# One engine instead of two empties PSUM, and the second pair of score tiles leaves in one store

## The chip, the core and the metric

The kernel runs on one NeuronCore of a Trainium2 chip; the other cores are idle. The metric is device microseconds (us) for one execution, as a median over several runs. The engines named below are PE (TensorE, matmuls), DVE (VectorE), ACT (ScalarE), POOL (GpSimd) and SP (SyncE, which here only issues DMAs). "SPq" and "ACTq" are the instruction queues of SP and ACT where they issue DMAs.

## The reference

```
q, k: (8, 8, 512, 64) float32          # batch, heads, seq, dim
out = einsum('bhqd,bhkd->bhqk', q, k) * (1 / sqrt(64))
out: (8, 8, 512, 512) float32
```

Each of the 64 batch-and-head pairs gives a 512 x 512 matrix of scaled dot products. There is no softmax. 16.78 MB are read and 67.11 MB are written, so the output is four times the input.

## The kernel before

**Tiles.** The work is cut into `ALL` = 16 tiles, numbered `g`. A tile is 4 MB of output: 16 matmuls of 128 x 512 results, in two rounds `x` of eight PSUM banks `i`. PSUM (`ps`) has eight banks of 128 x 512 float32, so one round fills all of PSUM. An evacuation takes four banks at once (`W` = 4, a 128 x 2048 block), multiplies by the scale and writes to SBUF. A tile has four evacuations, `n` = 0 to 3; `n` = 0 and 2 are the low four banks of the two rounds, `n` = 1 and 3 the high four.

**Buffers.** `big` in SBUF has `UNITS` = 4 slots of one tile each. Tile `g` goes to slot `g % 4`. The same four slots take the inputs first: all loads are issued at the start, one after another, to these slots (line 83, and two half loads at line 72). POOL casts them to bf16 in `xb` (line 126), DVE transposes them into `kT` (keys, line 191) and `qz` (queries, line 196) in eight sets `b` of two tiles each.

**Order on each engine.** Nothing is scheduled automatically; each engine has its own program, and semaphores tie them together.

- SP issues the loads and then the stores (lines 85 to 101). Tiles 0 to 3 are stored one by one (line 95): an even tile when PE has done the matmuls that imply its evacuation (`pe`), an odd tile when its last evacuation has counted `out` up. From tile 4 on two tiles leave in one store of 8 MB (line 98), issued when the odd one is done.
- PE runs a loop of four passes over four tiles each (lines 135 to 158). Before the first matmul of an even tile it waits for `free0` or `free1`, which counts that the store that used these two slots has landed, that the preceding pair has been evacuated, and that DVE has turned the operands. Within a tile, each four banks wait for their evacuation (`low0`, `low1`, `high0`, `high1`).
- ACT does all evacuations of tiles 0 to 3 and, from tile 4 on, those with `n` = 0, 2 and 3 (line 170).
- DVE does the evacuation `n` = 1 of tiles 4 to 15 (line 168), placed between its transposes: that of the even tile after the keys of a set, that of the odd tile between the second and third transpose of the queries, the last two at the end. The choice stands in `evacuate`:

```python
by_vector = g >= UNITS and n == 1
```

So two slots of `big` (a pair of tiles) are filled while the two other slots drain to memory.

Of the kernel before, what the change touches and what calls it, by code (L numbers as in the profile page):

```python
# [5 lines left out]
def kernel(  # L6
# [5 lines left out]
    nc = tc.nc  # L12
    B, H, S, D = q.shape
    scale = 1.0 / (D ** 0.5)
    P = 128
    Q = 32
    UNITS = B // 2
# [6 lines left out]
    W = 4  # L24
    ALL = 2 * B
# [11 lines left out]
    sem = {name: nc.alloc_semaphore(name) for name in names}  # L37
# [14 lines left out]
    bigs = [big[:, n] for n in range(UNITS)]  # L52
# [3 lines left out]
    ps = nc.alloc_psum_tensor("ps", [P, RO, S], f32)[:]  # L56
# [6 lines left out]
    def xf(v):  # L63
        return bigs[v].rearrange("p x i k -> p (x i k)").rearrange("p (x s c) -> p x s c", x=2, s=2)
# [6 lines left out]
    for s, queue in enumerate((nc.sync, nc.scalar)):  # L71
        first_load = queue.dma_start(
            out=xf(0)[:, 0, s].rearrange("p (x c) -> p x c", x=2), in_=k_0[s]
# [7 lines left out]
    for n in range(1, 2 * UNITS):  # L81
        v, x = divmod(n, 2)
        nc.sync.dma_start(out=xf(v)[:, x].rearrange("p s c -> p (s c)"), in_=(k_r, q_r)[x][v]
                          ).then_inc(load_sems[n], 16)
    for g in range(ALL):
        if g % 2:
            nc.sync.wait_ge(sem["out"], g // 2 + 1)
        elif g < UNITS:
            nc.sync.wait_ge(sem["pe"], 4 * g + 6)
        else:  # L90
            continue
        dst = out_r[g // 4, g // 2 % 2]
        free = sem[f"free{g // 2 % 2}"]
        if g < UNITS:
            nc.sync.dma_start(out=dst[:, g % 2 * 2:g % 2 * 2 + 2],  # L95
                              in_=bigs[g].rearrange("p x i k -> p x (i k)")).then_inc(free, 16)
        else:
            nc.sync.dma_start(out=dst, in_=big[:, g % UNITS - 1:g % UNITS + 1].rearrange(
                "p n x i k -> p (n x) (i k)")).then_inc(free, 32)
        if g % 2 and g < ALL - 1:  # L100
            nc.sync.sem_inc(sem[f"free{1 - g // 2 % 2}"], 1)  # L101
# [5 lines left out]
    for v in range(UNITS):  # L107
# [3 lines left out]
        for x in range(2):  # L111
            if v or x:
                nc.gpsimd.wait_ge(load_sems[2 * v + x], 16)
            for s in range(2):
                if v == x == 0:
                    nc.gpsimd.wait_ge(halves[s], 16)
                src = xf(v)[:, x, s]
                dst = xb[:, slot(v, x)]
                if x == 0:
                    src = src.rearrange("p (w e d) -> p w e d", e=2, d=D)  # L120
                    dst = dst[:, s * J // 2:(s + 1) * J // 2].rearrange("p w d e -> p w e d")
                else:
                    src = src.rearrange("p (jj e i d) -> p jj e i d", e=2, i=RO, d=D)
# [10 lines left out]
    pe = nc.tensor  # L134
    with pe.Fori(0, ALL // 4):
        for t in range(4):
# [10 lines left out]
            for x in range(2):  # L147
                for i in range(RO):
                    if (x, i) in waits:
                        name, count = waits[x, i]  # L150
# [5 lines left out]
                    elif (x, i) in takes:  # L156
                        name, count = takes[x, i]
                        ins.then_inc(sem[name], -count)


    def evacuate(g, n):
        x, i = n // 2, n % 2 * W
        by_vector = g >= UNITS and n == 1
        engine = nc.vector if by_vector else nc.scalar
        engine.wait_ge(sem["pe"], 4 * g + n + 1)
        to, src = bigs[g % UNITS][:, x, i:i + W], ps[:, i:i + W]
        if by_vector:
            freed = nc.vector.tensor_scalar_mul(out=to, in0=src, scalar1=scale)  # L168
        else:
            freed = nc.scalar.mul(out=to, in_=src, mul=scale)  # L170
        name = "out" if g % 2 and n == 3 else f"{('low', 'high')[n % 2]}{g // 2 % 2}"
        freed.then_inc(sem[name], 1)

    for g in range(ALL):
        for n in range(4):
            if g < UNITS or n != 1:
                evacuate(g, n)

# [1 line left out]
    def turn_keys(b, y, heads=slice(0, G)):  # L182
        s = b % 2 * 2 * Q
        out = kw[2 * y * Q:2 * (y + 1) * Q, b % 2 * G:(b % 2 + 1) * G]
        src = xw[s:s + 2 * Q, slot(b // 2, 0), :, y * Q:(y + 1) * Q]
        if b < 2:
            out = out[:, heads].rearrange("d g (m w) -> d g w m", m=Q)
            src = src.rearrange("p (g w) d -> p g w d", g=G)[:, heads]
        else:
            out = out.rearrange("d g (m w) -> d w m g", w=J)  # L190
        return nc.vector.transpose(out=out, in_=src)  # L191

    def turn_queries(b, y, h, rows=slice(0, RO)):
        s = (b % 2 * 2 + h) * Q
        d = (2 * y + h) * Q
        return nc.vector.transpose(  # L196
            out=qw[d:d + Q, b % 2 * G:(b % 2 + 1) * G, rows, h * Q:(h + 1) * Q].rearrange(
                "d g i (m jj) -> d i jj m g", jj=JJ),
            in_=xw[s:s + Q, slot(b // 2, 1), :, y * Q:(y + 1) * Q].rearrange(
                "p (i jj) d -> p i jj d", i=RO)[:, rows])  # L200

    sides = [(y, h) for y in range(2) for h in range(2)]
# [12 lines left out]
    for b in range(1, SETS):  # L215
        if b >= 2:
            nc.vector.wait_ge(sem["pe"], 8 * (b - 1))
        if b % 2 == 0:
            nc.vector.wait_ge(sem["ready"], b + 1)
        for y in range(2):  # L220
            turn_keys(b, y)
        if b > 2:
            evacuate(2 * b - 2, 1)
        if b % 2 == 0:
            nc.vector.wait_ge(sem["ready"], b + 2)
        for n, (y, h) in enumerate(sides):
            if b > 2 and n == 2:
                evacuate(2 * b - 1, 1)
            last = turn_queries(b, y, h)
        last.then_inc(sem["turned" if b == 1 else f"free{b % 2}"], 1)  # L230
    for g in (ALL - 2, ALL - 1):
        evacuate(g, 1)


# [28 lines left out]
```

## Time and profile before

| | us |
|---|---|
| median of 4 runs | 200.69 (200.49 to 200.76) |
| profiled execution, its own time | 200.51 |
| profiled execution, span from first to last instruction | 199.1 |

| engine | busy us | share of the span | what it does |
|---|---|---|---|
| DVE | 127.2 | 64% | 54 transposes, 12 evacuations, one memset |
| ACT | 95.9 | 48% | 52 evacuations |
| PE | 80.2 | 40% | matmuls |
| POOL | 38.9 | 20% | casts, all in the first quarter |
| DMA | | 99% of 16 engines (97.7% + 1.3%) | loads and stores, 421 GB/s over the span |

| group | mean ns of one | count |
|---|---|---|
| ACT evacuation, 128x2048 float32, line 170 | 1883 | 52 |
| DVE evacuation, 128x2048 float32, line 168 | 2292 | 12 |
| DVE transpose of queries, 32x1024, line 196 | 2014 | 28 |
| DVE transpose of keys, 64x1024, line 191 | 1932 | 14 |

The profile is of one execution. Busy time is summed over the span, and says nothing by itself of what holds up the end; the chain that ended last and the waits do. All DMA rows carry a share of the core's 16 DMA engines: near 1.00 means that all of them were moving data. The share can come out a little over 1 in a short stretch, because a packet is counted where it begins.

### The profile page before, as it was taken

Reading aid. Unit: us, or ns where it says so; the run is one execution under the profiler, and the core shown is the slowest. Engines: PE = TensorE matmul, PEld = TensorE weight load, DVE = VectorE, ACT = ScalarE, POOL = GpSimd, SP = SyncE. Lnnn points to the kernel's source line nnn. Section 1 sums busy time; section 2 is a strip of 40 time slices with the busy share of each in tenths; the row PEclk is TensorE's granted clock in tenths of the full one; section 3 lists DMA queues with packets and bytes.
Section 4 is the critical chain, followed back from the end, with each engine's and each line's share of the span. In section 5 each row is a group of like instructions: output and inputs, shape, how many; then the busy total and the mean of one; then the engine's idle time right before and its main releaser. Section 6 shows DMA issues by size and latency. Waiting matters only on the chain.

```text
span 199.1 us, 726 instructions
## 1 busy us (share of the span) xinstructions
PE 80.2 (40%) x252; PEld 23.6 (12%) x256; DVE 127.2 (64%) x67; ACT 95.9 (48%) x53; POOL 38.9 (20%) x20
## 2 busy tenths in 40 slices
PE   0000357556514752575167516660756076600000
PEld 0000021121101110221022102110211021100000
DVE  4248999999370799589959895999399513400000
ACT  2000049959960776177526752773377337720000
POOL 0399999698000000000000000000000000000000
PEclk9999999979995899589957975998599859955555
DMA  6999999999999999999999999999999999999997
GB/s 201 431 438 441 435 425 421 421 412 425 438 444 425 428 425 438 444 421 428 425 438 441 428 426 425 435 438 431 428 428 431 431 441 425 425 425 431 425 431 309
DMA packets 5809, 83.90 MB, mean 421 GB/s; under 512 B 304, under 2 KB 304, under 8 KB 816
## 3 DMA queue, kind: packets, MB, share of 16 engines
q1 hardware_dynamic: 5536, 82.84, 97.7%
q10 hardware_dynamic: 272, 1.05, 1.3%
q14 instruction: 1, 0.01, 0.0%
HBM read 16.78 MB, written 67.11 MB: 421 GB/s over the span
## 4 chain that ended last, share of the span: by engine, by line
DMA 41%; ACT 30%; PE 8%; DVE 4%; POOL 2%; issue 1%; SPq 0%
DMA out_dram<-big 36%; ACT big L170 30%; PE ps L152 8%; DMA big<-in_q_dram 6%; DVE qz L196 4%; POOL xb L126 2%; SPq L95 0%; SPq L101 0%
## 5 line engine op out<-in xcount | busy, mean ns | idle before, releaser
L170 ACT ACTIVATE big<-ps 128x2048 f32<-128x2048 f32 x52 | 94.6, 1883 | 77.8 <-PE ps L152 77.8
L152 PE MATMUL ps<-kT,qz 128*128 128x512 bf16 x252 | 80.2, 455 | 93.4 <-DMA out_dram<-big 37.1
L196 DVE STREAM_TRANSPOSE qz<-xb 32x1024 f32<-32x1024 f32 (+1 forms) x36 | 65.2, 1811 | 1.2 <-POOL xb L126 0.7
L168 DVE TENSOR_SCALAR big<-ps 128x2048 f32<-128x2048 f32 x12 | 27.5, 2292 | 30.2 <-PE ps L152 30.2
L152 PEld LDWEIGHTS ps<-kT,qz 128*128 128x128 bf16 x256 | 23.6, 110 | 149.5 <-DMA out_dram<-big 40.1
L126 POOL CAST xb<-big 128x2048 bf16<-128x2048 f32 x16 | 38.7, 2472 | 10.1 <-DMA big<-in_k_dram 7.5
L191 DVE STREAM_TRANSPOSE kT<-xb 64x1024 f32<-64x1024 f32 (+1 forms) x18 | 31.5, 1747 | 11.0 <-POOL xb L126 6.5
L203 DVE MEMSET qz<- 128x4096 uint32 x1 | 3.5, 3472 | 2.9 <-PEq L77 2.9
L170 ACT ACT_TABLE_LOAD x1 | 1.3, 1283 | 2.0 <-PEq L77 2.0
L247 POOL MEMSET const-float32-0.0<- 128x1 f32 x1 | 0.1, 99 | 0.2 <-issue 0.2
L247 POOL MEMSET const-bfloat16-1.0<- 128x1 bf16 x1 | 0.1, 102 | 0.0
L247 POOL MEMSET const-uint8-127<- 128x1 uint8 x1 | 0.1, 102 | 0.0
L247 POOL MEMSET const-float32-1.0<- 128x1 f32 x1 | 0.1, 99 | 0.0
## 6 DMA issues: line engine op xcount, KB each, us to landing
out_dram<-big SPq DMA_DIRECT2D x6, 8192.0 KB
out_dram<-big SPq DMA_DIRECT2D x4, 4096.0 KB
big<-in_q_dram SPq DMA_DIRECT2D x4, 2048.0 KB, 23.9
big<-in_k_dram SPq DMA_DIRECT2D x3, 2048.0 KB, 23.9
big<-in_k_dram SPq DMA_DIRECT2D x1, 1024.0 KB, 7.2
big<-in_k_dram ACTq DMA_DIRECT2D x1, 1024.0 KB, 8.7
```

The costliest lines, as they stand in the source:

```text
L126: cast = nc.gpsimd.tensor_copy(out=dst, in_=src)
L152: ins = pe.matmul(out=ps[:, i], lhsT=qz[:, 2 * t + x, i], rhs=kT[:, 2 * t + x], start=True, stop=True)
L168: freed = nc.vector.tensor_scalar_mul(out=to, in0=src, scalar1=scale)
L170: freed = nc.scalar.mul(out=to, in_=src, mul=scale)
L191: return nc.vector.transpose(out=out, in_=src)
L196: return nc.vector.transpose(out=qw[d:d + Q, b % 2 * G:(b % 2 + 1) * G, rows, h * Q:(h + 1) * Q].rearrange("d g i (m jj) -> d i jj m g", j ...
L203: nc.vector.memset(qz, 0.0).then_inc(sem["zeroed"], 1)
L247: nc = _bacc.Bacc("TRN2", target_bir_lowering=False, num_devices=1)
```

## The change

Tiles 2 and 3 leave in one store, as the later pairs do, so SP issues two single stores and seven pairs instead of four and six. All evacuations are done by ACT, in the order of tiles; those with `n` = 1 of tiles 4 to 15 move from DVE to ACT. DVE keeps the memset and the transposes, in the same order. The waits of the moved evacuations (on `pe`) and what they count up (`high0`, `high1` for the next wait of PE) are the same as before. Only the index of the first pair and the even tile's wait differ in SP's program: the wait for `pe` at tile 2 is gone.

```diff
     for g in range(ALL):
         if g % 2:
             nc.sync.wait_ge(sem["out"], g // 2 + 1)
-        elif g < UNITS:
+        elif g == 0:
             nc.sync.wait_ge(sem["pe"], 4 * g + 6)
         else:
             continue
         dst = out_r[g // 4, g // 2 % 2]
         free = sem[f"free{g // 2 % 2}"]
-        if g < UNITS:
+        if g < 2:
             nc.sync.dma_start(out=dst[:, g % 2 * 2:g % 2 * 2 + 2],
...
-    def evacuate(g, n):
-        x, i = n // 2, n % 2 * W
-        by_vector = g >= UNITS and n == 1
-        engine = nc.vector if by_vector else nc.scalar
-        engine.wait_ge(sem["pe"], 4 * g + n + 1)
-        to, src = bigs[g % UNITS][:, x, i:i + W], ps[:, i:i + W]
-        if by_vector:
-            freed = nc.vector.tensor_scalar_mul(out=to, in0=src, scalar1=scale)
-        else:
-            freed = nc.scalar.mul(out=to, in_=src, mul=scale)
-        name = "out" if g % 2 and n == 3 else f"{('low', 'high')[n % 2]}{g // 2 % 2}"
-        freed.then_inc(sem[name], 1)
-
     for g in range(ALL):
         for n in range(4):
-            if g < UNITS or n != 1:
-                evacuate(g, n)
+            x, i = n // 2, n % 2 * W
+            nc.scalar.wait_ge(sem["pe"], 4 * g + n + 1)
+            freed = nc.scalar.mul(out=bigs[g % UNITS][:, x, i:i + W], in_=ps[:, i:i + W], mul=scale)
+            name = "out" if g % 2 and n == 3 else f"{('low', 'high')[n % 2]}{g // 2 % 2}"
+            freed.then_inc(sem[name], 1)
...
         for y in range(2):
             turn_keys(b, y)
-        if b > 2:
-            evacuate(2 * b - 2, 1)
         if b % 2 == 0:
             nc.vector.wait_ge(sem["ready"], b + 2)
-        for n, (y, h) in enumerate(sides):
-            if b > 2 and n == 2:
-                evacuate(2 * b - 1, 1)
+        for y, h in sides:
             last = turn_queries(b, y, h)
         last.then_inc(sem["turned" if b == 1 else f"free{b % 2}"], 1)
-    for g in (ALL - 2, ALL - 1):
-        evacuate(g, 1)
```

## The prediction

> **What bounds the kernel now.** I read the page's slices first. All 16 DMA engines are busy from the second slice to the last but one, at 412 to 444 GB/s, while every compute engine has gaps.
>
> ```profile
> DMA  6999999999999999999999999999999999999997
> GB/s 201 431 438 441 435 425 421 421 412 425 438 444 425 428 425 438 444 421 428 425 438 441 428 426 425 435 438 431 428 428 431 431 441 425 425 425 431 425 431 309
> HBM read 16.78 MB, written 67.11 MB: 421 GB/s over the span
> ```
>
> The reader should see that no slice in the middle has a hole. 83.9 MB at the 432 GB/s of the middle are 194.2 us of a span of 199.1 us. So an engine's time counts only if it leaves the DMA engines without work. Whether it comes near to that is read from the chain that ended last.
>
> ```profile
> 81.84 1.90 PE ps L152 x4
> ...
> 93.67 3.65 ACT big L170 x2
> 97.32 0.02 issue
> 97.34 23.62 DMA out_dram<-big
> 120.96 0.05 issue
> 121.00 1.90 PE ps L152 x4
> ```
>
> A pair's round has three steps. PE starts when the store that used these two slots has landed (81.84). PSUM is filled and emptied eight times. Then SP issues the pair's store (97.34), which lands 23.62 us later. But 8.39 MB need only 19.4 us at 432 GB/s: the new store first queues behind the other pair's. That queueing is the reserve. To see how large it is I took the PE starts and the store issues from the timeline and asked for the stretch between them:
>
> ```profile
> 41.97:58.18 16.21, 9.69 (x31) 2.88 (x32) 12.02 (x7) 14.27 (x8) 7.28 (x4) 0.90 1.00 430
> 62.39:77.85 15.46, 9.66 (x32) 2.89 (x32) 11.60 (x6) 11.04 (x6) 0.00 (x0) 0.89 1.01 432
> 81.84:97.34 15.50, 10.02 (x31) 2.94 (x32) 12.35 (x7) 11.04 (x6) 0.00 (x0) 0.86 1.01 434
> 101.34:117.22 15.88, 10.55 (x32) 3.01 (x32) 12.34 (x7) 10.94 (x6) 0.00 (x0) 0.82 1.01 432
> 121.00:136.17 15.17, 9.43 (x31) 2.89 (x32) 12.57 (x7) 10.96 (x6) 0.00 (x0) 0.91 1.00 431
> 140.50:155.97 15.47, 9.66 (x32) 2.87 (x32) 11.97 (x7) 11.04 (x6) 0.00 (x0) 0.88 1.00 429
> 160.09:175.62 15.53, 10.15 (x31) 2.97 (x32) 4.58 (x2) 10.94 (x6) 0.00 (x0) 0.83 1.00 427
> ```
>
> Each row is a pair from its first matmul to its store's issue: start and end, length, busy time of PE, PEld, DVE, ACT and POOL, granted clock, DMA share, GB/s. The first row is tiles 2 and 3, which ACT already empties alone (x8); in the others ACT does six and DVE two. So the trace of before contains the changed stage. The starts are 19.45, 19.50, 19.66, 19.50 and 19.59 us apart (62.39, 81.84, 101.34, 121.00, 140.50, 160.09): the time that a pair takes to drain. The reserve, from an issue to the next start, is 3.99, 4.00, 3.78, 4.33 and 4.12 us.
>
> **The change, part by part.** *Twelve evacuations leave DVE.* 12 x 2.292 = 27.5 us go, and DVE's transposes of a set end earlier. They were in time already: the queries of the next pair end at 78.75 (74.73 + 4.02), PE starts at 81.84. Worth nothing; the 8.5 us that PE waits for DVE's evacuations turn into waits for ACT.
>
> *Twelve evacuations go to ACT.* 12 x 1.883 = 22.6 us are added in ACT's queue, two per pair, with the third and fourth evacuation of each tile behind them, and behind those PE's refill of the banks and the pair's store. ACT takes eight in a row in 14.27 us, one every 1.77 us, since one begins before the former has quite ended:
>
> ```profile
> 43.89 14.27 ACT L170 ACTIVATE big<-ps 128x2048 f32<-128x2048 f32 x8 [2.43 <-PE ps L152]
> ```
>
> With 1.92 us for the first four matmuls that makes the 16.21 us of the first row. That stage ran beside DVE transposes and POOL casts, at half clock in its first microseconds like the later ones, so I take it as it is. The difference to the other rows is 0.75, 0.71, 0.33, 1.04, 0.74 and 0.68 us, mean 0.71: the two engines overlap little, because PE can refill only four banks at a time. At worst, with no overlap of two ACT instructions, the stage is 1.92 + 8 x 1.883 = 16.98 us. At best it is as long as now.
>
> The Trainium skill speaks against the change here: "PSUM — Partial Sum Buffer", section "Specifications (TRN2)", says that ScalarE and VectorE can read PSUM in parallel at full bandwidth when they use different banks. By that rule alone a pair's 8 x 1.883 us could be halved by two engines, so that one alone would take 7.5 us longer per pair; this overruns the reserve by 3.5 us six times, some 21 us. The rows of 15.5 and 16.21 us show 0.7 us instead.
>
> *What covers it.* The reserve becomes 19.45 - 16.21 = 3.24 us for the narrowest pair, 2.47 us at worst (19.45 - 16.98). The path has no shorter cover than that: if it is too small, each pair's store begins late by the shortfall, the DMA engines idle for it, and the next pair starts late by as much. What a store needs before the landing of the one ahead can be bounded by both ends of the span. At the start, the first load is issued at 0.73 us; no byte moves up to 1.8 us, and the rate is full (410 GB/s) from 3.0 us: 1.1 to 2.3 us from issue to flow. At the end, the last packets begin at 197.8 to 198.1 us. A packet of a store is 16 KB (the `(i k)` of line 92), and one of 16 engines moves 432 / 16 = 27 GB/s, so it takes 0.61 us; the data end at 198.4 to 198.7 us, and the landing is seen at 199.06, 0.4 to 0.7 us later.
>
> ```profile
> 1.40:1.80 0.40, 0.00 (x0) 0.00 (x0) 0.00 (x0) 0.00 (x0) 0.00 (x0) 1.00 0.00 0
> 1.80:2.20 0.40, 0.00 (x0) 0.00 (x0) 0.00 (x0) 0.23 (x1) 0.00 (x0) 1.00 1.13 113
> ...
> 3.00:4.00 1.00, 0.00 (x0) 0.00 (x0) 1.00 (x1) 0.25 (x1) 0.00 (x0) 1.00 1.04 410
> ...
> 197.80:198.10 0.30, 0.00 (x0) 0.00 (x0) 0.00 (x0) 0.00 (x0) 0.00 (x0) 0.50 0.15 55
> ```
>
> So a store needs 1.5 to 3.0 us of lead before the landing. I take 2.0, nearer to the low end, since descriptors of a queued store can be made while data flows, and since a lead of 3.78 us shows a DMA share of 1.02 (117 to 121 us). 3.24 us is enough for all of that interval, 2.47 us for most of it. Cost taken: 0; with both worst ends 6 x (3.0 - 2.47) = 3.2 us. A gain is excluded in this term, since a later issue adds nothing to engines whose share is 1.00 already. The Trainium skill, "DMA: Bandwidth & Descriptors", section "Anatomy of one DMA", gives a fixed cost of about 2.0 us per transfer, fitted for another issuing path; by that too the lead would do, and no run here shows it for a store.
>
> *Tiles 2 and 3 as a pair.* SP loses one issue and one wait (for PE's matmuls) and the store of tile 2 moves from 52.2 us, where the timeline has its issue, to 58.18 us, where tile 3's is issued now. Nothing stands behind it but the store of tile 3 and the count for `free0`, which stay at 58.18. The DMA engines meanwhile work on tiles 0 and 1, which land at 62.34 (PE starts at 62.39): a lead of 4.16 us, more than the later pairs have. If this cover were gone it would cost its shortfall once. Tiles 2 and 3 drained by 81.79 as two stores, in 19.45 us, and pairs take 19.45 to 19.66. Shape can be worth the difference of the rates, 430 GB/s from 62 to 82 us and 432 from 82 to 160: 8.39 MB in 19.51 or 19.42 us. I take -0.05 us, between 0 and -0.09.
>
> *The last pair.* Its store is issued 0.7 us later (176.3), still 3 us before the pair ahead has landed. The chain's last step gets shorter, the end does not move.
>
> The sum: 200.51 (199.1 in the span, 1.4 around it) + 0 - 0.05 = 200.46 for an execution like the profiled one. That one lay 0.18 below the median of the runs, so the median should be 200.64; I say 200.6.
>
> **The rivals.** *Slower: the stores run dry.* ACT alone becomes the pair's bound when 16.2 to 17.0 us of filling plus the lead exceed the 19.5 us of draining; it decides from a needed lead of 3.24 us, or of 2.47 us if ACT instructions do not overlap. For it: the reserve shrinks by a fifth, and its other side is only bounded. Against it: the row of 41.97 to 58.18 is a measured length, not an estimate. Half of the worst shortfall, 0.27 us, six times: 1.6 us, 202.2 us. Chance 0.10, and 0.03 for small losses, such as one DMA engine that ends a little later than the others.
>
> *Faster: the stores flow better.* Fewer bytes of VectorE traffic beside the DMA reads of SBUF, and more even DMA engines at the end. For it: with all engines idle (180 to 190 us) the rate is 434, against 432 in the middle; 0.5% of the 137 us from 62 us on is 0.6 us, and the slower stretch of 41 to 62 us (427 GB/s) could give 0.25 more: 199.8 at most. Against it: ACT takes over 22.6 of the 27.5 us, so only a part can go. Half of it: 200.2 us. Chance 0.20.
>
> *The change gives what its DVE numbers suggest.* If DVE's 127 us were the bound, 27.5 us less would be felt. It isn't: PE's waits at pair starts are all for DMA (37.1 us, six times). Less than 0.01.
>
> **How the numbers follow.** Forecast, no change: 0.67, at 200.6 us. Changes under 0.2%, 0.4 us, are about what a measurement of this kernel can't tell from none; the bounds are 200.29 and 201.09. Faster 0.20, slower 0.13. The range goes from 200.1, which holds half of the faster case, to 201.3, which leaves out the greater part of the dry case (202.2).
>
> **What would show it.** Right: in the changed profile every ACT stretch of a pair is some 16.2 us, the PE starts stay 19.5 us apart, the wait of PE for stores falls from 37.1 us by some 6 x 0.7 us to 33, the DMA share is 1.00 at each issue, DVE busy falls to about 100 us and ACT rises to 118. Wrong: a DMA share below 0.95 in the two microseconds ahead of a PE start, pairs over 19.8 us apart, or a rate in the middle other than 430 to 434 GB/s.

## The result, and the profile after

The changed kernel takes 200.38 us (median of 39 runs, 200.24 to 200.81), the kernel before 200.66 us (59 runs, 200.47 to 200.93). The ratio is 0.9988, with a 95% interval of 0.9984 to 0.9993: a gain of 0.12%, inside the band that was called no change, but not zero. The profiled execution took 200.32 us, with a span of 199.0.

The slices of the changed kernel's page, DMA busy tenths and rate:

```profile
DMA  6999999999999999999999999999999999999997
GB/s 198 435 428 458 425 428 422 422 418 425 438 435 428 431 425 438 431 431 428 431 430 435 431 430 431 425 438 435 425 435 428 435 431 428 435 428 425 425 422 320
```

There is still no hole. The stretches of the seven pairs that fill `big`, from the first matmul to the store's issue (start and end, length, busy time of PE, PEld, DVE, ACT and POOL, clock, DMA share, GB/s), in the changed kernel:

```profile
41.98:58.23 16.25, 10.33 (x31) 2.99 (x32) 11.97 (x7) 14.30 (x8) 7.23 (x4) 0.82 1.00 428
62.29:78.62 16.33, 10.46 (x32) 3.01 (x32) 7.78 (x5) 14.37 (x8) 0.00 (x0) 0.81 1.01 431
81.74:97.95 16.21, 9.44 (x31) 2.89 (x32) 8.70 (x6) 14.27 (x8) 0.00 (x0) 0.91 1.01 432
101.28:117.49 16.21, 9.81 (x32) 2.89 (x32) 8.49 (x6) 14.27 (x8) 0.00 (x0) 0.88 1.01 433
120.83:137.05 16.22, 10.16 (x31) 2.95 (x32) 8.50 (x6) 14.27 (x8) 0.00 (x0) 0.82 1.01 434
140.40:156.93 16.53, 10.55 (x32) 3.02 (x32) 6.04 (x4) 14.37 (x8) 0.00 (x0) 0.81 1.01 431
160.00:176.22 16.22, 9.57 (x31) 2.87 (x32) 0.00 (x0) 14.27 (x8) 0.00 (x0) 0.91 1.00 427
```

The reader should see eight evacuations on ACT in every row (x8), a fill of 16.2 to 16.5 us where it was 15.2 to 15.9, and the DMA share at 1.00 all the same. PE starts of neighbouring pairs are 19.45, 19.54, 19.56, 19.58 and 19.59 us apart, as before (the fifth pair's first matmul is at 140.42). The reserve, from an issue to the next start, is now 3.12, 3.32, 3.34, 3.37 and 3.07 us. The two microseconds ahead of two of the starts, where a dry queue would show first (same columns; all six starts have a share of 0.96 to 1.02):

```profile
79.74:81.74 2.00, 0.00 (x1) 0.01 (x1) 1.99 (x2) 0.00 (x0) 0.00 (x0) 0.50 1.02 434
118.83:120.83 2.00, 0.00 (x0) 0.00 (x0) 1.99 (x2) 0.00 (x0) 0.00 (x0) 0.50 0.96 410
```

The chain that ended last of the changed kernel shows what became of the 0.7 us per pair: the fill is longer, the store's step shorter (22.84 us instead of 23.62 from issue to landing), and the next start is where it was.

```profile
81.74 1.90 PE ps L152 x4
83.64 0.02 issue
83.66 14.28 ACT big L165 x8
97.94 0.02 issue
97.95 22.84 DMA out_dram<-big
120.79 0.05 issue
120.83 1.90 PE ps L152 x4
```

So the mechanism is the forecast's. What is left to explain is the 0.28 us, of which the prediction had 0.05. Subtracting the span from the time, run by run, shows where they are: 1.33 us lie outside the span (mean of 41 runs of the changed kernel), against 1.50 us for the kernel before (21 runs beside the first four experiments), while the mean spans are 199.10 and 199.14 us. By the means of these runs the time falls by 0.22 us (200.64 to 200.42), and 0.17 of it is not in the span at all. "Outside" below means the difference of time and span.

### The profile page after: what moved, and what is told of

Read it like the earlier page. It is cut to its first block, busy times and chain, and to the rows that moved or that the text cites. A ratio compares the mean times of both kernels' runs of the same rounds, so it can differ in the third digit from the quotient of the medians.

```text
span 199.0 us, 725 instructions
## 1 busy us (share of the span) xinstructions
PE 80.7 (41%) x252; PEld 23.7 (12%) x256; DVE 100.1 (50%) x55; ACT 115.8 (58%) x65; POOL 38.9 (20%) x20
## 4 chain that ended last, share of the span: by engine, by line
DMA 40%; ACT 35%; PE 5%; DVE 4%; POOL 2%; issue 0%; SPq 0%
ACT big L165 35%; DMA out_dram<-big 35%; DMA big<-in_q_dram 6%; PE ps L152 5%; DVE qz L186 4%; POOL xb L126 2%; SPq L95 0%; SPq L101 0%
## 5 line engine op out<-in xcount | busy, mean ns | idle before, releaser
L165 ACT ACTIVATE big<-ps 128x2048 f32<-128x2048 f32 x64 | 114.5, 1900 | 58.5 <-PE ps L152 58.5
L152 PE MATMUL ps<-kT,qz 128*128 128x512 bf16 x252 | 80.7, 456 | 93.0 <-DMA out_dram<-big 35.1
```

What stands on the lines that cost most here:

```text
L152: ins = pe.matmul(out=ps[:, i], lhsT=qz[:, 2 * t + x, i], rhs=kT[:, 2 * t + x], start=True, stop=True)
L165: freed = nc.scalar.mul(out=bigs[g % UNITS][:, x, i:i + W], in_=ps[:, i:i + W], mul=scale)
```

## The experiments

### Which half of the change gains

The pair store alone, on the kernel before:

```diff
-        elif g < UNITS:
+        elif g == 0:
             nc.sync.wait_ge(sem["pe"], 4 * g + 6)
...
-        if g < UNITS:
+        if g < 2:
```

> Only the store of tiles 2 and 3 is joined; VectorE keeps its 12 evacuations. Theory 1 (the 0.28 us come from one store fewer, with its issue and its 16 completions): some 0.2 us faster than before, 200.4 us. Theory 2 (they come from VectorE, which no longer writes its 12 evacuations beside the stores): as before, 200.65 us, at most 0.05 us less. In both, the stretches from a pair's first matmul to its store's issue stay near 15.5 us.

Measured: 200.62 us beside 200.62, ratio 0.9998 (0.9989 to 1.0007), outside 1.51.

The evacuations alone: the changed kernel with those two conditions put back.

> Only the evacuations move to ScalarE; tiles 2 and 3 are stored singly as before. Theory 1 (one store fewer): as before, 200.65 us. Theory 2 (less VectorE traffic): some 0.2 us faster, 200.4 us. If the gain is the sum of two small ones, both this and the run with the pair alone lie half way, near 200.5 us. In all, the stretches of the pairs are 16.2 us and the store's reserve 3.2 us.

Measured: 200.42 us, ratio 0.9989 (0.9980 to 0.9998), outside 1.31, mean span 199.12. The move of the evacuations carries the gain; joining the store carries none that is measured. But theory 2, that DVE's writes slow the stores, would have shortened the span, and the span hardly moved: both theories are in trouble.

### What the gain is

The queue that the profile calls "instruction" differs between the two pages (packets, MB and share, within the span). Of the kernel before:

```profile
q14 instruction: 1, 0.01, 0.0%
```

Of the changed kernel:

```profile
q14 instruction: 2, 0.02, 0.0%
```

In the packet records of the trace, the kernel before has one 8 KB instruction packet at 116.78 us and another at 200.34 us, after the last instruction of the span; the changed kernel has them at 100.29 and 117.84 us and none after the end. Theory A: an engine's program crosses the end of a block of instructions; with more instructions in front it asks for the next block while the stores run, where it would cost nothing, and not at the end, where it would. ACT's program grew from 52 evacuations to 64, DVE's shrank by 12. Two kernels tell these apart. The first leaves the kernel before as it is and adds 12 fillers to ACT:

```diff
         engine.wait_ge(sem["pe"], 4 * g + n + 1)
         to, src = bigs[g % UNITS][:, x, i:i + W], ps[:, i:i + W]
+        if g >= UNITS and n == 2:
+            nc.scalar.mul(out=spare[:, g:g + 1], in_=ps[:, i, 0:1], mul=scale)
```

> The kernel before with nothing of the change, but ScalarE does 12 more instructions of one column each (128x1, into a spare tile), one ahead of the third evacuation of each tile from 4 on. ScalarE thus has as many instructions as in the changed kernel, VectorE keeps its 12 evacuations. Theory A (the gain is an instruction fetch that a longer ScalarE program does within the span instead of after it): the time outside the span falls from 1.50 to 1.32 us, the page counts two instruction packets within the span instead of one, and the time is 200.4 us although work was added. Theory B (it is VectorE's shorter program, or its traffic): 200.6 us, outside 1.50.

Measured: 200.47 us beside 200.60, ratio 0.9992 (0.9983 to 1.0001); outside 1.33, and two instruction packets:

```profile
q14 instruction: 2, 0.02, 0.0%
```

The ratio alone would not decide it, since its interval just takes in 1; the time outside does (1.33 here, 1.50 in 28 runs of the kernel before beside it). Twelve useless instructions, 171 ns each, make the kernel before as fast outside the span as the changed one. The second puts work back on DVE in the changed kernel:

```diff
         for y in range(2):
             turn_keys(b, y)
+        if b > 2:
+            fill(2 * b - 6)       # wait for the fill before, then memset(spare), 128x1920 float32
...
-        for y, h in sides:
+        for n, (y, h) in enumerate(sides):
+            if b > 2 and n == 2:
+                fill(2 * b - 5)
```

> The changed kernel, in which VectorE fills a spare tile of 128x1920 float32 at each of the 12 places where its evacuations stood (with a wait of its own for the fill before). VectorE writes to SBUF and counts instructions nearly as before. Theory A (ScalarE's longer program): 200.4 us, 1.32 us outside the span. Theory B (VectorE's shorter program): 200.6 us, 1.50 outside. Theory 2 (VectorE's traffic slows the stores): 200.6 us, but with the span longer by 0.2 us and 1.32 outside.

Measured: 200.45 us, outside 1.34, mean span 199.12. (There are ten fills, not twelve; the last two evacuations, behind all transposes, were not replaced. Ten of 1.66 us are 16.6 us of writing.) DVE's traffic costs nothing that is seen, and its shorter program is not needed for the gain. Two more, to close the table: 12 one-column fillers on DVE, and 6 instead of 12 on ACT, both on the kernel before.

```diff
         if by_vector:
+            nc.vector.memset(spare[:, g:g + 1], 0.0)
             freed = nc.vector.tensor_scalar_mul(out=to, in0=src, scalar1=scale)
```

> The kernel before with 12 more instructions of one column (128x1, into a spare tile) on VectorE, one ahead of each of its evacuations; ScalarE's program stays at 52 evacuations. If the fetch that moved belongs to ScalarE's program, nothing changes: 200.6 us, 1.50 us outside the span, one instruction packet within it. If any longer program does it, or the whole kernel's size, 200.4 us, 1.32 outside and two packets.

Measured: 200.64 us beside 200.59, ratio 1.0004 (0.9994 to 1.0014), outside 1.48, one packet.

```diff
-        if g >= UNITS and n == 2:
+        if g >= UNITS and g % 2 == 0 and n == 2:
```

> The kernel before with 6 instead of 12 more one-column instructions on ScalarE, one ahead of the third evacuation of each even tile from 4 on: 58 evacuations and fillers. If the fetch comes within the span as soon as ScalarE's program passes a block's end, this lands on one of the two levels, 1.32 us outside with two packets or 1.50 with one, and nothing between them (1.41); it tells on which side of 58 the end lies.

Measured: 200.49 us beside 200.59, ratio 0.9993 (0.9983 to 1.0003), outside 1.33, two packets.

| kernel | ACT evacuations and fillers | DVE evacuations and fillers | instruction packets in the span | outside, us |
|---|---|---|---|---|
| before | 52 | 12 | 1 | 1.50 |
| before, three evacuations of each pair on DVE (below) | 46 | 18 | 1 | 1.57 |
| pair store alone | 52 | 12 | 1 | 1.51 |
| before, 12 fillers on DVE | 52 | 24 | 1 | 1.48 |
| before, 6 fillers on ACT | 58 | 12 | 2 | 1.33 |
| before, 12 fillers on ACT | 64 | 12 | 2 | 1.33 |
| evacuations alone | 64 | 0 | 2 | 1.31 |
| changed | 64 | 0 | 2 | 1.33 |
| changed, 10 fills on DVE | 64 | 10 | 2 | 1.34 |

ACT's count alone separates the rows: 1.48 to 1.57 us up to 52, 1.31 to 1.34 from 58 on. The four kernels below that are built on the changed one, with 64 to 76, also have two packets and 1.32 to 1.34 us. So it is shown that the length of ACT's program sets the 0.17 us.

That the late packet is what costs them is argued, not shown. For it: three profiled executions have such a packet (kernel before, pair store alone, 12 fillers on DVE); it begins 1.28 to 1.31 us after the last instruction, and where it takes longer, 0.32, 0.34 and 0.40 us, the time outside is longer too, 1.36, 1.41 and 1.45 us. Against it: the kernel with 46 evacuations on ACT has no packet after the end in its trace, and still 1.57 us outside (1.53 in the nine runs of the kernel before beside it). Nor does the record say whose program a packet belongs to. The rest of the gain, 0.05 us of span by the means, can't be told from none.

### How much reserve there is

The prediction's slower rival needed a number that the trace of before only bounded: how much ahead of the landing of one store the next must be issued. Here ACT repeats the last evacuation of each of the six later pairs, once or twice, so that the stores come later. (A repeat writes the same values and goes ahead of the real evacuation, which waits on a semaphore for it.)

```diff
+            for again in range(1 if g > UNITS and g % 2 and n == 3 else 0):   # 2 for two repeats
+                nc.scalar.mul(out=bigs[g % UNITS][:, x, i:i + W], in_=ps[:, i:i + W], mul=scale
+                              ).then_inc(sem["again"], 1)
+                nc.scalar.wait_ge(sem["again"], 1 * (g // 2 - 2) + again + 1)
             freed = nc.scalar.mul(out=bigs[g % UNITS][:, x, i:i + W], in_=ps[:, i:i + W], mul=scale)
```

> The changed kernel, in which ScalarE does the last evacuation of each of the six later pairs twice (same data to the same place), so that each store is issued some 1.9 to 2.0 us later. The reserve falls from 3.2 to some 1.3 us. If a store needs a lead of 1.5 to 3.0 us before the landing of the one ahead, as the prediction bounded it, with 2.0 taken, the time grows by 6 x 0.7 = 4 us, to 204.5 us, and by 1 to 10 us at the bounds; a DMA share below 1 shows ahead of each PE start. If it needs less than 1.3 us, the time stays at 200.4 us.

Measured: 202.47 us (202.02 to 202.72), ratio 1.0088 (1.0072 to 1.0104), 2.1 us above the changed kernel: half of the 4 us expected with the lead that was taken, and within the bounds of 1 to 10. The dry moments show in the windows ahead of the starts, of the run with one repeat:

```profile
80.90:82.00 1.10, 0.00 (x0) 0.00 (x0) 1.10 (x1) 0.01 (x1) 0.00 (x0) 0.50 0.67 283
121.00:122.00 1.00, 0.00 (x0) 0.00 (x0) 1.00 (x1) 0.00 (x0) 0.00 (x0) 0.50 0.70 295
141.00:141.80 0.80, 0.03 (x1) 0.04 (x2) 0.80 (x1) 0.00 (x0) 0.00 (x0) 0.50 0.78 328
```

The DMA share is 0.67 to 0.78 there, where the changed kernel has 0.96 to 1.02.

> As the run with one repeat, with two: each of the six stores is issued some 3.9 us later than in the changed kernel, and the reserve of 3.2 us is gone (-0.7 us). With a lead of 2.0 us the time grows by 6 x 2.7 = 16 us, to 216.5 us; with 1.5 us by 13, with 3.0 us by 22. If the stores were not what sets the pace, the added 6 x 3.9 = 23 us of ScalarE would show in full, or not at all.

Measured: 208.75 us (208.49 to 208.90), ratio 1.0401 (1.0385 to 1.0417), 8.4 us above the changed kernel: the direction right, the size half. The issue of the first of these stores, and the windows around it, of the run with two repeats:

```profile
82.55 0.40 SPq L98 DMA_DIRECT2D out_dram<-big  x1
```

```profile
81.50:82.50 1.00, 0.00 (x0) 0.00 (x0) 0.99 (x2) 1.00 (x1) 0.00 (x0) 0.50 0.00 0
82.50:83.50 1.00, 0.45 (x2) 0.18 (x3) 1.00 (x1) 0.02 (x1) 0.00 (x0) 0.50 0.27 115
83.50:84.50 1.00, 1.00 (x4) 0.39 (x3) 0.99 (x2) 0.00 (x0) 0.00 (x0) 0.50 0.96 410
```

From 81.5 to 82.5 us nothing moves, the store is issued at 82.55, and the rate is full from about 83.6: in the packet records the first packet begins 0.90 to 0.91 us after the issue, and all 16 engines run after 1.06 us, here and in the two stores that follow (issues at 103.08 and 124.16). Issue to full flow is thus 1.06 us for a store, just under the 1.1 to 2.3 us that the prediction read from the first load. With 0.4 to 0.7 us from the end of the data to the landing, the lead needed is 1.5 to 1.8 us, not the 2.0 that was taken.

Why the expectation of 16 us was double: it charged the missing reserve and the lead to each of six pairs. With two repeats the fill is so long that the store ahead has landed before the pair is full, and PE then starts the next pair 0.5 us after the issue, when SP has counted up its semaphore behind the issue (line 101), not after a landing. (In brackets, PE's idle time before and what ended it.)

```profile
83.05 3.54 PE L152 MATMUL ps<-kT,qz 128*128 128x512 bf16 x8 [6.79 <-SPq L101]
104.12 3.25 PE L152 MATMUL ps<-kT,qz 128*128 128x512 bf16 x8 [7.33 <-SPq L101]
124.70 3.20 PE L152 MATMUL ps<-kT,qz 128*128 128x512 bf16 x8 [6.83 <-SPq L101]
```

The second of these starts came 1.04 us after its issue (103.08), since one DMA engine's last landing was as late as 104.08. The starts are 20.5 to 21.1 us apart, about the fill of 20.0 us plus 0.5. ACT's fill has become the bound; against the 19.55 us of before that is 1.2 us per pair, some 7 us for six, and the lead is paid once.

A finer step, half of an evacuation repeated (`i:i + 2` in place of `i:i + W`):

> The changed kernel, with half of the last evacuation (128x1024) of each later pair done twice: each store is issued some 1.0 us later, the reserve is some 2.2 us. From the two runs with full repeats a store flows 1.04 us after its issue, and a landing is seen 0.45 us after the data end, so a store needs 1.5 us of lead. Then this one costs nothing: 200.4 us, DMA share 1.00 at all PE starts. If a lead of 2.0 us was needed as the prediction took, the reserve of 2.2 is still enough, and with the upper bound, 3.0 us, the time grows by some 4 us.

Measured: 200.72 us (200.55 to 201.16), ratio 1.0011 (1.0002 to 1.0021), 0.34 us above the changed kernel, with a mean span of 199.46 us. The reserve was 2.19, 2.16, 2.60, 1.85 and 2.28 us (issues at 79.63, 99.09, 118.52, 138.65 and 157.78 us, next starts at 81.82, 101.25, 121.12, 140.50 and 160.06). So a reserve over 1.8 us did not come free, and this expectation missed. The narrowest one shows, in the run with half a repeat:

```profile
138.50:140.50 2.00, 0.00 (x0) 0.00 (x0) 1.99 (x2) 0.13 (x1) 0.00 (x0) 0.50 0.95 393
```

In the packet records only 7 of the 16 engines were moving data at the worst moment between 139.5 and 140.1 us. The engines do not end a store together (the 16 landings of the five stores ahead of these starts lie 0.3 to 0.8 us apart), so those in front run dry before the last. Why that costs the last engine 0.3 us as well stays open. The edge is soft: nothing is lost at 3.1 to 3.4 us of reserve, 0.3 us in all at 1.9 to 2.6, and 2.1 us with one full repeat, which was to leave 1.3 (its profile has 1.1 to 2.2, because a store that starts late also lands late).

### Two attempts that were slower

The other way round: three of the eight evacuations on DVE.

```diff
-        by_vector = g >= UNITS and n == 1
+        by_vector = g >= UNITS and n in (1, 3)[:2 - g % 2]
...
             evacuate(2 * b - 2, 1)
+            evacuate(2 * b - 2, 3)
```

> The kernel before, turned the other way: VectorE does three of the eight evacuations of each later pair (the third one being the even tile's last), ScalarE five. By the row of before a second evacuation on VectorE shortened the fill from 16.21 to 15.5 us; by the rule that both engines read PSUM in parallel a third would shorten it by some 1.9 us more, to 13.6. If instead an evacuation on VectorE (2.29 us) just takes the place of one of ScalarE (1.77 us) in a chain that hardly overlaps, the fill stays near 15 to 16.5 us. In both cases the stores set the pace: span as before, 199.1 us, and 200.6 us with 1.50 us outside the span, since ScalarE's program is shorter still (46 evacuations).

Measured: 205.75 us (205.46 to 206.01), ratio 1.0255 (1.0241 to 1.0269), where 200.6 was expected. The fill grew to 19.45 us (62.48 to 81.93) instead of shrinking. Both expectations missed what stands in DVE's queue. DVE and PE in that kernel, from the timeline:

```profile
71.74 4.00 DVE L196 STREAM_TRANSPOSE qz<-xb 32x1024 f32<-32x1024 f32 x2
75.75 2.29 DVE L168 TENSOR_SCALAR big<-ps 128x2048 f32<-128x2048 f32 x1
```

```profile
78.10 1.46 PE L152 MATMUL ps<-kT,qz 128*128 128x512 bf16 x3 [4.28 <-DVE big L168]
```

The odd tile's evacuation stands behind two transposes (4.00 us) and starts at 75.75, and PE waits 4.28 us for it. In the kernel before it started at 72.41, 0.2 us after the second transpose. The last pair of this run has no transposes left in DVE's queue, and its row, in the columns of above, shows what they cost:

```profile
164.54:180.35 15.81, 10.42 (x32) 3.02 (x32) 6.88 (x3) 9.39 (x5) 0.00 (x0) 0.82 1.00 427
```

The fill is 15.81 us there, not 19.45: the transposes are what made it long. But it is no shorter than the 15.53 us of the kernel before's last pair, with two evacuations on DVE and no transposes either: a third evacuation on DVE buys nothing in this chain.

The first keys in one transfer, on the changed kernel, to be sooner at full rate:

```diff
-    for s, queue in enumerate((nc.sync, nc.scalar)):
-        first_load = queue.dma_start(
-            out=xf(0)[:, 0, s].rearrange("p (x c) -> p x c", x=2), in_=k_0[s]
-        ).then_inc(halves[s], 16)
+    first_load = nc.sync.dma_start(
+        out=xf(0)[:, 0].rearrange("p s c -> p (s c)"), in_=k_r[0]).then_inc(load_sems[0], 16)
...
-        if b < 2:
-            out = out[:, heads].rearrange("d g (m w) -> d g w m", m=Q)
-            src = src.rearrange("p (g w) d -> p g w d", g=G)[:, heads]
-        else:
-            out = out.rearrange("d g (m w) -> d w m g", w=J)
+        out = out.rearrange("d g (m w) -> d w m g", w=J)
```

> The changed kernel with the first keys loaded by one 2 MB transfer in the layout of the later loads (16 KB packets) instead of two of 1 MB with 4 KB packets on two queues; the transposes of the first two sets take the form of the later ones. If the DMA engines set the time, what counts is how soon they are at full rate: the windows before 3 us show 113 to 215 GB/s, and 410 from then to 12 us against 426 later. 2 MB at 426 instead of 410 GB/s are 0.2 us; with the first microsecond at full rate up to 0.5 more. 199.9 to 200.2 us. If the pace of the first tiles counts instead, it is unchanged or slower.

Measured: 201.19 us (200.92 to 201.56), ratio 1.0028 (1.0016 to 1.0041), 0.8 us slower than the changed kernel, where 199.9 to 200.2 was expected. The loss is where the loads end and the stores begin. This kernel:

```profile
36.00:43.00 7.00, 3.18 (x11) 1.03 (x12) 6.94 (x4) 5.38 (x4) 5.39 (x3) 0.93 0.99 344
```

The changed kernel, same window:

```profile
36.00:43.00 7.00, 3.09 (x11) 1.04 (x12) 6.94 (x4) 5.47 (x4) 5.13 (x3) 0.80 0.99 410
```

The share is 0.99 in both, but packets take longer (a tenth of the 16 KB packets over 1.14 us, against 0.65 in the changed kernel), and 66 GB/s over 7 us are 0.46 MB or 1.1 us. The other eleven profiles, all with the old first load, have 377 to 421 GB/s in this window, so the handover also varies by itself. Why it is slower still with this load is open.

## Why the prediction was right, and where its sizes were off

- **The bound.** DMA share 1.00 and starts 19.5 us apart were the forecast and are there. With the reserve taken away the same kernel shows holes and lost time, so the reserve is what hid the longer fill: shown, not only argued.
- **The longer fill.** 16.21 us was read from the pair that ACT had emptied alone; the changed pairs take 16.2 to 16.5. The prediction rests on this row of before. By its estimate from the Trainium skill's rule on parallel reads ("PSUM — Partial Sum Buffer", "Specifications (TRN2)") the loss was to be some 21 us; the 0.7 us of the row was right for this chain. The traces do not speak against the rule itself: an evacuation on DVE takes 2.29 us in all 12 cases of the kernel before, also where ACT reads the other four banks at the same time. The estimate left out that an evacuation has to wait for PE's refill of its banks, and those come in order: in the last pair with three on DVE, where no transposes stand in the way, 16.27 us of evacuations (9.39 on ACT, 6.88 on DVE) still take 13.9 us from the first to the last.
- **The lead.** Taken as 2.0 us from a range of 1.5 to 3.0; issue to full flow is 1.06 us, so 1.5 to 1.8 us in all for a queue that has run dry, while the first 0.3 us are lost at reserves of 1.9 to 2.6. The forecast did not depend on it, since 3.1 us were left. The rival's price did: "the shortfall six times" is right only while the landing sets the next start, not when the fill itself becomes the bound.
- **The joined store.** -0.05 us was taken, and the run with the pair alone gives 200.62 beside 200.62, with an interval too wide to tell 0.05 us. The landings tell more: tiles 2 and 3 drain in 19.45 us as one store (62.24 to 81.69) as they did as two (62.34 to 81.79). No effect of shape is seen.
- **The term that was missing.** The sum carried 1.4 us around the span unchanged from one kernel to the other. It falls by 0.17 us, because ACT's program is longer; nothing in the forecast looked there. That is most of the way from 200.6 to 200.38. The faster rival had the sign of the result, but not the mechanism: less VectorE traffic gained nothing (the ten fills cost nothing), and it was to show in the span.
- **Smaller sizes.** PE's wait for stores fell from 37.1 to 35.1 us, not to 33: the last matmuls of a pair end only some 0.35 us later (76.15 instead of 75.80 in the first of the later pairs), and the rest of the longer fill lies behind them, in the last evacuations. ACT is busy for 115.8 us (118 forecast), DVE for 100.1 (100).

## What to carry to other kernels

When the DMA engines are full, ask of an engine's change only whether the next transfer is still issued early enough: read the reserve from the issue of one to the landing of the one ahead, and compare it with the measured time from issue to flow. Look for a stretch of the old trace that already runs in the new way; its length is better than any sum. And when the time moves by tenths while the span does not, look outside the span, at what the program's length does.

## What the hardware showed that was not expected

- Twelve, or six, useless one-column instructions on ACT take 0.17 us off the time outside the span (1.33 instead of 1.50 us), and an 8 KB instruction packet that came after the end comes within the run. Twelve on DVE do nothing (1.48). That the packet is the cause is not shown.
- An evacuation on DVE takes 2.29 us whether or not ACT reads other banks of PSUM at the time (18 in the run with three of eight on DVE, with none to 1.22 us of overlap).
- The first packet of a store begins 0.90 us after its issue and all 16 DMA engines move data after 1.06 us, in three issues onto a dry queue.
- Where loads hand over to stores, 36 to 43 us, the same DMA share (0.99) moved 410 GB/s in one kernel and 344 in another whose first load has another layout.
